# Prompt scores as paired products of 64 rows, and the last pair of gate and up joined inside the down projection

## The chip, the cores and the metric

The kernel runs on one core of a Trainium2 chip. The metric is the device time of one execution in microseconds; the kernel before has a median of 2318.37 us over three runs (2318.06 to 2319.26). The names of the engines are those of the profile: PE is the matrix engine (PEld its weight loads), DVE the vector engine, ACT the scalar engine, POOL and SP the two engines that here issue most transfers (POOL through the software queue q0, SP through the hardware queue q1).

## The reference, cut to what matters

One step of a decoder of two layers, in float32, for a prompt of 1024 positions and eight samples of one position each with 2048 cached positions. Layer 0 mixes with an S5 recurrence and a differential attention, layer 1 with a gated recurrence and pooling; each layer ends with a SwiGLU. The two parts that matter:

```python
# attention of the prompt: 4 heads, each with two components of 64 dimensions
s = jnp.einsum('bqhd,bkhd->bhqk', qblk, k)          # per component
p = jax.nn.softmax(where(causal, s, -inf))
w = p[:, :, 0] - lam * p[:, :, 1]                   # component 0 minus lam times component 1
o = jnp.einsum('bhqk,bkhe->bqhe', w, v)

# each layer's feed-forward part, 1024 -> 2816 -> 1024
return (jax.nn.silu(x @ wg) * (x @ wu)) @ wd
```

The prompt and the samples go through the feed-forward part together: 1024 + 8 = 1032 columns.

## The kernel before

Every large product is made of three products of operands split into a high and a low part (high by high, low by high, high by low), which is what lines 718 to 720 issue. The feed-forward products go further and use a scheme of seven products for a 2 by 2 block. A program of its own sorts the instructions of each engine ahead of the run; each engine then takes its row of instructions in that order and waits in place where an operand isn't there yet.

**The prompt's attention** (some 290 us of the run, from 330 to 620 us) is worked through in eight rounds: four heads with the first 512 query rows (G=0), then the four heads with the second 512 (G=1). A round has four groups of 128 query rows (qi 0 to 3); group qi of round G looks at nk = (4G + qi + 1) * 128 keys, in blocks of at most 512. `attn_load` fetches the q and k of the next round while the current one runs; it is a generator, and `LOADS` says how many of its steps are taken ahead of each group. In memory a head's q and k lie as one high and one low matrix each (`qd[h][i]`, `kd[h][i]`), whose 128 rows are the 64 dimensions of component 0 and, below them, the 64 of component 1. Before, the Q tile holds for each component the high part of q in its upper 64 rows and the low part in its lower 64; KH and KL hold one component's high (low) part of k twice, in the upper and the lower 64 rows (at G=0 both lie in a tile K). So one product of 128 rows by KH gives qh·kh + ql·kh, and one by KL gives qh·kl + ql·kl. `attn_scores` issues these two per block and component (L1308, L1309), then adds the causal mask with a product in bfloat16 (L1311). At G=0 the two components share one PSUM tile of the pool `sc`; at G=1 each has its own, and the pool has two. DVE takes the maxima (L1313 at G=1, L1317 at G=0), ACT the exponentials (L1319); `attn_values` subtracts the components, transposes (L1338) and multiplies by v (L1348).

The same stage carries, in between, the eight samples' attention over the cached values: SP loads pages kv of 256 KB into eight buffers, and PE multiplies them (`so`, L1453). It also carries the output projection: POOL loads residual rows xr and stores the sums xp, ao and az to memory, and its queue is first in, first out; the q and k loads stand in that queue as well.

**The feed-forward part.** `gate_up` makes eleven pairs of gate and up products; after each pair `finish` multiplies the up half by the norm's factors (`normed`, two operations on L404) and joins it with the gate half (two on L409), all four on DVE with 1032 columns each. For the first ten pairs the result goes to memory; the last stays in its tiles `self.last`, which `down` stores when it loads the rest of the residual (`load_x(8)`). `down` begins with operands built on DVE (b, L476 and the sums beside it) and weight sums as and wp: L515 makes the low part of each weight wp. An item is 24 products of PE with one wp.

Of the kernel before, what the change touches and what calls it, by code (L numbers as in the profile page):

```python
# [8 lines left out]
F32 = mybir.dt.float32  # L9
F32R = mybir.dt.float32r  # L10
# [3 lines left out]
ALU = mybir.AluOpType  # L14
AX = mybir.AxisListType
# [18 lines left out]
P, D = "gpsimd", "vector"  # L34
# [23 lines left out]
NB = 16 // NI  # L58
QUEUES = ("gpsimd", "sync", "sync", "gpsimd", "gpsimd")
Y_BUFS = 11  # L60
LOADS = (2, 2, 2, 2)
MID = 4
KV_BUFS = 8
DENSE = (1, 1, 1, 1, 1, 1, 1, 1)
# [132 lines left out]
class Ffn:  # L197
# [180 lines left out]
    def gate_up(self, S, pp):  # L378
        t, nc = self.t, self.t.nc
        pa = t.pd  # L380

        def slots(j):
            return [t.tile("c", pool=None if j else S) for _ in range(2)] + [None, None, set()]
# [18 lines left out]
        def normed(c):  # L402
            for x in c[:2]:
                nc.vector.tensor_tensor(x, x, t.R, ALU.mult)  # L404

        def finish(j, g, u):
            normed(u)
            for i in range(2):
                self.lastf = nc.vector.tensor_tensor(g[i], g[i], u[i], ALU.mult)  # L409
                if j < 10:  # L410
                    nc.gpsimd.dma_start(self.hd[2 * j + i], g[i])
            self.last = g

        cg, cu = slots(0), slots(0)
# [33 lines left out]
        for j in range(1, 11):  # L448
            cg, cu = slots(j), slots(j)
            for v, c in ((0, cg), (1, cu)):  # L450
                w = self.load(v, j, S if v else t.wst)
                got = nxt[2 * j - 2 + v] if 2 * j - 2 + v < AHEAD else None
                for p in ORDER:
                    if p != 2 or got is None:
                        self.product(p, w, c, pp, got=got if p == 1 else None)
                if self.l + v == 0 and j == 5:
                    with t.after(self.lastf):
                        t.lru_consts()
                if v == 0:
                    normed(cg)  # L460
                    for x in cg[:2]:
                        nc.scalar.activation(x, x, AF.Silu)
            finish(j, cg, cu)

    def operands(self, h, grp, S):

# [51 lines left out]
    def down(self, xs, S, pp, chunks):  # L518


        t, nc = self.t, self.t.nc
# [69 lines left out]
        def load_x(n):  # L591
            for m in range(len(xs), n):
                xs.append(t.tile(f"x{m}"))
                nc.sync.dma_start(xs[m], self.xd[m])
# [16 lines left out]
        def prep():  # L611
            ci, grp, p, m = weights.pop(0)
            ms = (m, m + 2) if grp and m % 4 == 0 else (m,)
            for j, mm in enumerate(ms):
                if (ci, grp, mm) not in raws:
                    raws[ci, grp, mm] = raw(ci, mm, grp, j), {}
            if ci + grp == 0 and m == 2 and len(xs) < 8:
                load_x(8)
                for j in range(2):
                    nc.sync.dma_start(self.hd[20 + j], self.last[j])  # L620
            made[ci, grp, p, m] = self.down_weights(p, *raws[ci, grp, m])

        bank, now = {}, None
        for n, (ci, grp, p, m, more) in enumerate(items):
# [6 lines left out]
            last = ci == chunks[-1] and grp == 1  # L631
# [8 lines left out]
class Trunk:  # L640
# [314 lines left out]
    def mixer0(self):  # L955
        tc, nc, a = self.tc, self.nc, self.a
        with ExitStack() as es:
# [17 lines left out]
            with tc.tile_pool(name="smp", bufs=1) as self.kv, ExitStack() as es5:  # L975
# [54 lines left out]
                with tc.tile_pool(name="mix", bufs=8) as self.T:  # L1030
# [9 lines left out]
                    for i, (h, G) in enumerate(order):  # L1040
                        nxt = loads[order[i + 1]] if i < 7 else iter(())
                        for qi in range(4):
                            for _ in range(LOADS[qi]):
                                next(nxt, None)
# [218 lines left out]
    def attn_load(self, h, G):  # L1263

        nc = self.nc
        n = 512 * G + 512
        self.qk = getattr(self, "qk", {})
        Q = self.tile("Q", F32R)[:, :1024].rearrange("p (c n) -> p c n", c=2)
        ks = []
        self.qk[h, G] = (Q, ks)  # L1270
        for half in range(2):
            src = self.qd[h][half][:, G * 512:G * 512 + 512].bitcast(F32R).rearrange("(c p) n -> p c n", c=2)
            nc.gpsimd.dma_start(Q[half * 64:half * 64 + 64], src)
        yield
        for c in range(2):
            if G:
                ks.append([self.tile(t, F32R)[:, :n] for t in ("KH", "KL")])
            else:
                t = self.tile("K", F32R)
                ks.append([t[:, 0:512], t[:, 512:1024]])  # L1280
            for i in range(2):
                for half in range(2):
                    nc.gpsimd.dma_start(ks[c][i][half * 64:half * 64 + 64],
                                        self.kd[h][i][c * 64:c * 64 + 64, :n].bitcast(F32R))
                yield

    def attn_scores(self, h, G, qi):

        nc = self.nc
        Q, ks = self.qk[h, G]  # L1290
        if qi == 0:
            self.sums = getattr(self, "sums", {})
            self.sums[h, G] = self.sm.tile([128, 2, 4], F32, tag="sums", name="sums")
        sm = self.sums[h, G][:, :, qi]
        nk = (4 * G + qi + 1) * 128
        mx = self.sm.tile([128, 2], F32, tag="mx", name="mx")
        both = None if G else self.sc.tile([128, 2, 512], F32, tag="sc", name="sc")
        P2 = None if G else self.tile("P")
        S, P = [], []
        for c in range(2):  # L1300
            KH, KL = ks[c]
            ql = Q[:, c, qi * 128:qi * 128 + 128]
            ps = self.sc.tile([128, 1024], F32, tag="sc", name="sc") if G else both[:, c]
            for k0 in range(0, nk, 512):
                n = min(512, nk - k0)
                last = k0 + n == nk
                o = ps[:, k0:k0 + n]
                nc.tensor.matmul(o, ql, KH[:, k0:k0 + n], start=True, stop=False)  # L1308
                nc.tensor.matmul(o, ql, KL[:, k0:k0 + n], start=False, stop=not last)  # L1309
                if last:  # L1310
                    nc.tensor.matmul(o[:, n - 128:n], self.identb, self.maskb, start=False, stop=True)  # L1311
            if G:
                nc.vector.tensor_reduce(mx[:, c:c + 1], ps[:, :nk], AX.X, ALU.max, negate=True)  # L1313
            S.append(ps[:, :nk])
            P.append(self.tile(f"P{c}")[:, :nk] if G else P2[:, c * 512:c * 512 + nk])
        if not G:
            nc.vector.tensor_reduce(mx, both[:, :, :nk], AX.X, ALU.max, negate=True)  # L1317
        for c in range(2):
            nc.scalar.activation(P[c], S[c], AF.Exp, bias=mx[:, c:c + 1], accum_out=sm[:, c:c + 1])  # L1319
        return P  # L1320
# [729 lines left out]
```

## Time and profile before

| | us |
|---|---|
| median of three runs | 2318.37 |
| profiled execution | 2323.5 |
| its span | 2321.7 |
| PE busy | 2192.2 (94%) |
| DVE busy | 1605.3 (69%) |
| ACT busy | 939.3 (40%) |
| POOL busy | 477.4 (21%) |

A row of the profile gives the busy time of a group of instructions, their mean duration, and the idle time ahead of them with what ended it. A wait is put down to the releaser that came last. Windows give busy time and the granted clock of PE in a stretch (1.00 is 2.4 GHz, 0.50 is 1.2 GHz). Matrix products overlap their neighbours, so what one costs is read from the distance between two starts and not from its duration.

### The profile page before, as it was taken

The numbers are of one execution on the slowest core, as the hardware profiler recorded it, in microseconds if no ns is written. First come the engines' busy times: TensorE is split into PE (matmuls) and PEld (weight loads), VectorE is DVE, ScalarE is ACT, GpSimd is POOL, SyncE is SP. The second block draws the span as 40 slices with busy tenths as digits, with TensorE's granted clock in tenths as the row PEclk, the third lists the DMA queues.
The fourth block names the chain that finished last, engine by engine and source line by source line (L and its number), as shares of the span: only waits on it lengthen the run. The fifth ranks groups of instructions, "written<-read, shape, count | busy, mean of one in ns | idle before, by whom it ended". The sixth has DMA issues, their size and how long they took to land.

```text
span 2321.7 us, 44913 instructions
## 1 busy us (share of the span) xinstructions
PE 2192.2 (94%) x17529; PEld 2061.1 (89%) x17529; DVE 1605.3 (69%) x3045; ACT 939.3 (40%) x1746; POOL 477.4 (21%) x585
## 2 busy tenths in 40 slices
PE   6999888887989999999899999999999999989998
PEld 6978766655789999999899998899899999989997
DVE  7879435445687557566999878654956565689966
ACT  5233234333664333333444365543633333344331
POOL 5232322222103333332000000000233333300001
PEclk8999998988999999999999999999999999999999
DMA  6488978998543222222765331334232122266512
GB/s 225 144 262 290 258 227 250 280 272 223 183 152 128 91 74 83 68 82 90 292 218 167 104 84 42 102 114 138 76 107 83 67 82 83 74 239 218 192 64 74
DMA packets 145798, 348.21 MB, mean 150 GB/s; under 512 B 33513, under 2 KB 40554, under 8 KB 145586
## 3 DMA queue, kind: packets, MB, share of 16 engines
q1 hardware_dynamic: 112514, 247.18, 32.4%
q0 software_dynamic: 32496, 97.64, 13.6%
q8 instruction: 138, 2.26, 0.4%
q14 instruction: 74, 0.61, 0.1%
q10 hardware_dynamic: 576, 0.52, 0.1%
HBM read 281.17 MB, written 64.08 MB: 149 GB/s over the span
## 4 chain that ended last, share of the span: by engine, by line
PE 79%; DVE 9%; DMA 7%; ACT 2%; issue 2%; SPq 1%; POOL 1%; DVEq 0%; ACTq 0%; POOLq 0%
PE pd L718 23%; PE pd L720 22%; PE pd L719 22%; DMA kv<-in_cv 3%; DMA kv<-in_ck 2%; PE so L1453 1%; PE po L1348 1%; PE pss L1402 1%; DVE wp L312 1%; DMA xr<-in_x 1%; PE pg L1918 1%; PE pT L1338 1%; PE sc L1308 1%; PE pv L1253 1%; PE pv L1254 1%
## 5 line engine op out<-in xcount | busy, mean ns | idle before, releaser
L720 PE MATMUL pd<-b,wp 128*128 128x256 f32 (+1 forms) x3496 | 987.7, 283 | 14.4 <-DVE wp L515 13.2
L718 PE MATMUL pd<-b,wp 128*128 128x256 f32 (+1 forms) x3496 | 991.7, 284 | 7.6 <-DVE c L373 3.5
L719 PE MATMUL pd<-b,wp 128*128 128x256 f32 (+1 forms) x3496 | 990.7, 283 | 2.3 <-DVE b L275 2.3
L720 PEld LDWEIGHTS pd<-b,wp 128*128 128x128 f32 x3496 | 662.3, 190 | 15.4 <-DVE wp L515 13.6
L718 PEld LDWEIGHTS pd<-b,wp 128*128 128x128 f32 x3496 | 662.6, 190 | 11.0 <-ACT wp L311 3.4
L719 PEld LDWEIGHTS pd<-b,wp 128*128 128x128 f32 x3496 | 662.8, 190 | 3.1 <-DVE b L275 3.1
L331 POOL TENSOR_TENSOR as<-wst 128x512 f32<-128x512 f32 x80 | 136.2, 1702 | 487.5 <-DVE wp L312 328.2
L718 PE MATMUL pd<-xh,wh 128*128 128x344 f32 x576 | 191.1, 333 | 14.7 <-ACT wh L691 10.2
L375 ACT COPY c<-pd 128x512 f32<-128x512 f32 (+1 forms) x260 | 106.1, 444 | 223.0 <-PE pd L720 222.7
L720 PE MATMUL pd<-xh,wl 128*128 128x344 f32 x576 | 188.1, 329 | 4.8 <-DVE wl L692 4.7
L719 PE MATMUL pd<-xl,wh 128*128 128x344 f32 x576 | 188.6, 328 | 0.0
L373 DVE TENSOR_TENSOR c<-pd,c 128x512 f32<-128x512 f32 (+1 forms) x214 | 93.3, 470 | 127.0 <-PE pd L720 126.8
L311 ACT CAST wp<-as 128x512 fp32r<-128x512 f32 x176 | 108.8, 621 | 173.0 <-PE pd L720 164.5
L312 DVE TENSOR_TENSOR wp<-wst,wp 128x512 fp32r<-128x512 f32 x122 | 105.4, 867 | 103.7 <-ACT wp L311 103.7
L312 DVE TENSOR_TENSOR wp<-as,wp 128x512 fp32r<-128x512 f32 x176 | 140.3, 800 | 28.0 <-ACT wp L311 27.9
L404 DVE TENSOR_TENSOR c<-c,R 128x1032 f32<-128x1032 f32 x88 | 110.4, 1255 | 44.9 <-ACT c L375 44.9
L718 PEld LDWEIGHTS pd<-xh,wh 128*128 128x128 f32 x576 | 110.0, 191 | 19.3 <-ACT wh L691 10.6
L583 DVE TENSOR_TENSOR x<-pd,x 128x512 f32<-128x512 f32 x160 | 108.3, 688 | 17.1 <-PE pd L720 15.8
L720 PEld LDWEIGHTS pd<-xh,wl 128*128 128x128 f32 x576 | 109.5, 191 | 8.7 <-DVE wl L692 5.9
L719 PEld LDWEIGHTS pd<-xl,wh 128*128 128x128 f32 x576 | 109.9, 191 | 2.1 <-issue 0.2
L691 ACT CAST wh<-wst 128x1024 fp32r<-128x1024 f32 x58 | 60.7, 1046 | 116.7 <-PE pd L719 85.4
L692 DVE TENSOR_TENSOR wl<-wst,wh 128x1024 fp32r<-128x1024 f32 x58 | 70.8, 1221 | 48.3 <-ACT wh L691 47.9
(537 smaller groups left out, 4075.1 us busy)
## 6 DMA issues: line engine op xcount, KB each, us to landing
h<-hd SPq DMA_DIRECT2D x82, 516.0 KB, 5.8
kv<-in_ck SPq DMA_DIRECT2D x128, 256.0 KB, 4.2
kv<-in_cv SPq DMA_DIRECT2D x128, 256.0 KB, 6.1
wst<-in_w_d SPq DMA_DIRECT2D x48, 512.0 KB, 4.2
wst<-in_w_g SPq DMA_DIRECT2D x46, 512.0 KB, 4.1
wst<-in_w_up SPq DMA_DIRECT2D x44, 512.0 KB, 3.5
hd<-c POOLq DMA_DIRECT2D x40, 516.0 KB, 3.0
wst<-in_w_o POOLq DMA_DIRECT2D x28, 512.0 KB, 4.0
```

The source lines that it names most:

```text
L311: nc.scalar.copy(W[:, 0], s)
L312: nc.vector.tensor_tensor(W[:, 1], s, W[:, 0].bitcast(F32), ALU.subtract)
L331: (nc.vector if self.first else nc.gpsimd).tensor_tensor(s, x, y, op)
L373: V.tensor_tensor(o, i, o, ALU.add)
L375: A.copy(o, i)
L404: nc.vector.tensor_tensor(x, x, t.R, ALU.mult)
L583: nc.vector.tensor_tensor(y, pt[:, :, :256], y, add)
L691: nc.scalar.copy(H, src)
L692: nc.vector.tensor_tensor(L, src, H.bitcast(F32), ALU.subtract)
L718: mm(p, WH, XH, start=first, stop=False, **kw)
L719: mm(p, WH, XL, start=False, stop=False, **kw)
L720: mm(p, WL, XH, start=False, stop=last, **kw)
```

## The change

In attention, q and k are loaded as they lie in memory: two loads of 128 rows for Q and two for K, where there were two for Q and eight for K. One K tile at G=0 and two at G=1 serve both components. The scores of a block are three products of 64 rows for each component (qh·kh, ql·kh, qh·kl); component 0 uses the upper 64 rows of the array and component 1 the lower 64, and the code issues them in turn. The two masks come at the end. At G=1 both PSUM tiles are taken at once. `LOADS` goes from two steps a group to one; a round has four steps now, one load each, so that the second load of k is asked for in the last group of the round before. In the feed-forward part `finish(10)` is called in `down`, just ahead of `load_x(8)` and the two stores, in both layers.

```diff
-LOADS = (2, 2, 2, 2)
+LOADS = (1, 1, 1, 1)
...
-            finish(j, cg, cu)
+            if j < 10:
+                finish(j, cg, cu)
+        self.finish = lambda: finish(10, cg, cu)
...
             if ci + grp == 0 and m == 2 and len(xs) < 8:
+                self.finish()
                 load_x(8)
...
+        for i in range(2):
+            nc.gpsimd.dma_start(Q[:, i], self.qd[h][i][:, G * 512:G * 512 + 512].bitcast(F32R))
+            yield
+            nc.gpsimd.dma_start(ks[i], self.kd[h][i][:, :n].bitcast(F32R))
+            yield
...
+        for k0 in range(0, nk, 512):
+            n = min(512, nk - k0)
+            last = k0 + n == nk
+            for j, (q, k) in enumerate(((0, KH), (1, KH), (0, KL))):
+                for c in range(2):
+                    r = slice(64 * c, 64 * c + 64)
+                    calls.append(lambda c=c, r=r, q=q, k=k, j=j, k0=k0, n=n, last=last: nc.tensor.matmul(
+                        S[c][:, k0:k0 + n], Q[r, q, sl], k[r, k0:k0 + n], start=j == 0, stop=j == 2 and not last))
         for c in range(2):
...
+            calls.append(lambda c=c: nc.tensor.matmul(S[c][:, nk - 128:nk], self.identb, self.maskb, start=False, stop=True))
+        self.row(calls)
```

`self.row(calls)` asks the sorting program to keep the calls together behind the first one. What it makes of that is seen in the order of the instructions. PE, round G=1 of head 0, last group but one (nk = 896), before; sc is the score tile of one component:

```order
L1308 MATMUL sc_7505<-KH_6898,Q_6895 128x512 [waits Activation_49]
L1309 MATMUL sc_7505<-KL_6899,Q_6895 128x512
L1308 MATMUL sc_7505<-KH_6898,Q_6895 128x384
...
L1309 MATMUL sc_7505<-KL_6899,Q_6895 128x384
...
L1311 MATMUL sc_7505<-maskb_684,identb_686 128x128
L1308 MATMUL sc_7513<-KH_7022,Q_6895 128x512
L1309 MATMUL sc_7513<-KL_7023,Q_6895 128x512
```

and the same group now, where lines have moved by one to three (L1308 and L1309 are now L1310, L1311 is L1313):

```order
L1310 MATMUL sc_7501<-KH_6894,Q_6893 128x512 [waits Activation_49]
L1310 MATMUL sc_7501<-KH_6894,Q_6893 128x512
L1310 MATMUL sc_7501<-KL_6895,Q_6893 128x512
L1310 MATMUL sc_7502<-KH_6894,Q_6893 128x512 [waits Activation_49]
L1310 MATMUL sc_7502<-KH_6894,Q_6893 128x512
L1310 MATMUL sc_7502<-KL_6895,Q_6893 128x512
L1310 MATMUL sc_7501<-KH_6894,Q_6893 128x384
L1310 MATMUL sc_7502<-KH_6894,Q_6893 128x384
```

The first block stands as three products of one component and then three of the other; the second stands in turn. At G=0 all groups stand in turn.

POOL's queue around the start of round G=1 of head 0, before (ao, xp are stores of the attention's output and of the sums, xr loads of the residual, wst weights of the output projection):

```order
L1356 DMA ao2_114<-od_6796 128x512 [waits DMASW6_49,DVE_49]
L1846 DMA xp3_119<-xr_6865 128x1032 [waits DMASW7_49]
L1836 DMA xr_7100<-in_x 128x1032 [waits DMASW0_49,PE_49]
L1283 DMA KL_7023<-kd0_108 64x1024 [waits DMASW1_49]
L1283 DMA KL_7023<-kd0_108 64x1024 [waits DMASW2_49]
L696 DMA wst_9060<-in_w_o0 128x1024 [waits DMASW3_49,Activation_49]
```

and now:

```order
L1838 DMA xr_7094<-in_x 128x1032 [waits DMASW3_49,PE_49]
L1358 DMA ao2_114<-od_6794 128x512 [waits DMASW4_49,DVE_49]
L1838 DMA xr_7213<-in_x 128x1032 [waits PE_49]
L1848 DMA xp4_120<-xr_7094 128x1032 [waits DMASW6_49,DMASW3_49,DVE_49]
L1281 DMA KL_6895<-kd0_108 128x1024 [waits DMASW7_49]
```

The residual load has moved ahead of the store ao2; the load of KL has moved behind a store xp4 that waits for DVE.

DVE at the passage from gate and up to down in layer 0, before (c are the gate and up tiles, wp the weights of down):

```order
L404 TENSOR_TENSOR c_14250<-c_14250,R_139 128x1032 [waits DVE_49]
L484 TENSOR_TENSOR h_14714<-h_14714,h_14712 128x520
L409 TENSOR_TENSOR c_14248<-c_14248,c_14250 128x1032 [waits DVE_49]
L404 TENSOR_TENSOR c_14251<-c_14251,R_139 128x1032 [waits Activation_49]
L476 TENSOR_TENSOR b_14745<-h_14714,b_14745 128x520 [waits Activation_49]
L409 TENSOR_TENSOR c_14249<-c_14249,c_14251 128x1032 [waits DVE_49]
L476 TENSOR_TENSOR b_14752<-h_14732,b_14752 128x512 [waits DMAHW1_49,Activation_49]
L476 TENSOR_TENSOR b_14755<-h_14732,b_14755 128x520 [waits Activation_49]
L482 TENSOR_TENSOR h_14730<-h_14730 128x512 [waits DMAHW0_49]
L515 TENSOR_TENSOR wp_14782<-as_14780,wp_14782 128x512
```

and now, from the first wp of down to its fifth (L515 is now L517, L476 is L478, L583 is L585):

```order
L517 TENSOR_TENSOR wp_14814<-as_14812,wp_14814 128x512
...
L478 TENSOR_TENSOR b_14795<-h_14764,b_14795 128x520 [waits Activation_49]
L517 TENSOR_TENSOR wp_14825<-as_14823,wp_14825 128x512 [waits PE_49]
L404 TENSOR_TENSOR c_14286<-c_14286,R_139 128x1032
L404 TENSOR_TENSOR c_14287<-c_14287,R_139 128x1032
L409 TENSOR_TENSOR c_14284<-c_14284,c_14286 128x1032 [waits DVE_49]
L585 TENSOR_TENSOR x1_14800<-pd_14828,x1_14800 128x512 [waits DMAHW7_49,PE_49]
L409 TENSOR_TENSOR c_14285<-c_14285,c_14287 128x1032 [waits DVE_49]
...
L517 TENSOR_TENSOR wp_14876<-as_14874,wp_14876 128x512 [waits Activation_49]
```

The four operations of the join have moved from ahead of the first wp to between the fourth and the fifth.

## Rows read from the trace of the kernel before

**Rows 1.** Windows of the attention stage: length, busy time by engine, PEclk, DMA share, GB/s

```profile
330.00:460.00 130.00, 106.58 (x638) 76.22 (x631) 63.05 (x155) 49.13 (x133) 36.34 (x65) 0.91 0.96 266
460.00:620.00 160.00, 132.99 (x760) 92.88 (x759) 87.07 (x193) 67.42 (x159) 37.46 (x69) 0.90 0.77 215
```

**Rows 2.** Waits of PE in 330 to 620 us: us in total, times, longest us

```profile
PE so L1453 <- DMA kv<-in_cv: 40.8, 10, 11.6
PE sc L1308 <- ACT P L1319: 4.1, 5, 1.5
```

**Rows 3.** Chain of waits, 330 to 620 us: shares by line, and one piece

```profile
by line: DMA kv<-in_cv 20.7%; PE po L1348 9.0%; PE so L1453 8.8%; PE pd L718 8.1%; PE pd L719 7.5%; PE pd L720 7.2%; DMA xr<-in_x 5.2%; PE sc L1308 5.0%; PE pT L1338 5.0%; PE sc L1309 3.9%; PE psn L801 2.6%; DMA K<-kd 2.2%; issue 2.1%; ACT 
...
458.76 8.06 DMA xr<-in_x
```

**Rows 4.** Transfers issued in 330 to 620 us: count, KB each, median us to landing

```profile
DMA packets 30360, 68.85 MB, mean 237 GB/s; under 512 B 4280, under 2 KB 4280, under 8 KB 30335
...
KH<-kd POOLq DMA_DIRECT2D x16, 256.0 KB, 9.0
KL<-kd POOLq DMA_DIRECT2D x16, 256.0 KB, 9.9
...
K<-kd POOLq DMA_DIRECT2D x24, 128.0 KB, 7.6
```

**Rows 5.** Timeline of PE, a score group at G=1: start, duration, line, tiles

```profile
481.91 0.48 PE L1308 MATMUL sc<-KH,Q 128*128 128x512 f32 x1
482.23 0.40 PE L1309 MATMUL sc<-KL,Q 128*128 128x512 f32 x1
482.47 0.28 PE L1308 MATMUL sc<-KH,Q 128*128 128x256 f32 x1
```

**Rows 6.** Timeline of PE in the S5 part: products of 64 rows

```profile
215.27 0.50 PE L1786 MATMUL py<-H,CL 64*128 64x136 f32 x4
215.70 1.08 PE L1402 MATMUL pss<-kv,qsam 128*32 128x128 f32 x32
216.87 0.50 PE L1788 MATMUL py<-H,CL 64*128 64x136 f32 x2
217.29 0.50 PE L1785 MATMUL py<-U,TG 128*128 128x136 f32 x2
```

**Rows 7.** Waits of POOL's queue in 330 to 620 us

```profile
POOL ao L1356 <- DVE sums L1332: 17.5, 1, 17.5
```

**Rows 8.** Waits of PE in 1090 to 1160 us

```profile
PE pd L720 <- DVE wp L515: 6.6, 1, 6.6
```

**Rows 9.** Page, costliest groups: count | busy, mean ns | idle before, releaser

```profile
L720 PE MATMUL pd<-b,wp 128*128 128x256 f32 (+1 forms) x3496 | 987.7, 283 | 14.4 <-DVE wp L515 13.2
```

**Rows 10.** Timeline of DVE, layer 0, the end of gate and up and the start of down

```profile
1116.22 1.23 DVE L404 TENSOR_TENSOR c<-c,R 128x1032 f32<-128x1032 f32 x1
...
1120.87 1.23 DVE L409 TENSOR_TENSOR c<-c 128x1032 f32<-128x1032 f32 x1
...
1123.82 0.69 DVE L515 TENSOR_TENSOR wp<-as,wp 128x512 fp32r<-128x512 f32 x1
...
1131.07 0.69 DVE L515 TENSOR_TENSOR wp<-as,wp 128x512 fp32r<-128x512 f32 x1
```

**Rows 11.** Timeline of PE at the same passage

```profile
1117.70 0.28 PE L719 MATMUL pd<-b,wp 128*128 128x256 f32 x1
1124.57 0.58 PE L720 MATMUL pd<-b,wp 128*128 128x256 f32 x1 [6.59 <-DVE wp L515]
...
1134.90 0.28 PE L718 MATMUL pd<-b,wp 128*128 128x264 f32 x1
1135.02 0.28 PE L719 MATMUL pd<-b,wp 128*128 128x264 f32 x1
```

**Rows 12.** Window behind that wait, columns as in Rows 1

```profile
1125.00:1130.00 5.00, 5.00 (x30) 5.00 (x30) 5.00 (x10) 0.62 (x1) 0.00 (x0) 0.65 0.99 376
```

More of the change, by code (lines that the diff above doesn't have):

```diff
@@ L1267, in attn_load @@
         self.qk = getattr(self, "qk", {})
-        Q = self.tile("Q", F32R)[:, :1024].rearrange("p (c n) -> p c n", c=2)
-        ks = []
-        self.qk[h, G] = (Q, ks)
[L1271 to L1285, printed above, removed]
+        Q = self.tile("Q", F32R)[:, :1024].rearrange("p (i n) -> p i n", i=2)
+        if G:
+            ks = [self.tile(t, F32R)[:, :n] for t in ("KH", "KL")]
+        else:
+            t = self.tile("K", F32R)
+            ks = [t[:, 0:512], t[:, 512:1024]]
+        self.qk[h, G] = (Q, ks)
+        for i in range(2):
[3 more added lines that the diff above has]
+            yield
     def attn_scores(self, h, G, qi):
         nc = self.nc
-        Q, ks = self.qk[h, G]
+        Q, (KH, KL) = self.qk[h, G]
         if qi == 0:
@@ L1296, in attn_scores @@
         mx = self.sm.tile([128, 2], F32, tag="mx", name="mx")
-        both = None if G else self.sc.tile([128, 2, 512], F32, tag="sc", name="sc")
-        P2 = None if G else self.tile("P")
-        S, P = [], []
-        for c in range(2):
[L1301 to L1315, printed above, removed]
@@ L1316, in attn_scores @@
-        if not G:
+        if G:
+            S = [self.sc.tile([128, 1024], F32, tag="sc", name="sc")[:, :nk] for _ in range(2)]
+            P = [self.tile(f"P{c}")[:, :nk] for c in range(2)]
+        else:
+            both, P2 = self.sc.tile([128, 2, 512], F32, tag="sc", name="sc"), self.tile("P")
+            S = [both[:, c, :nk] for c in range(2)]
+            P = [P2[:, c * 512:c * 512 + nk] for c in range(2)]
+        sl = slice(qi * 128, qi * 128 + 128)
+        calls = []
+        for k0 in range(0, nk, 512):
[6 more added lines that the diff above has]
+                        S[c][:, k0:k0 + n], Q[r, q, sl], k[r, k0:k0 + n], start=j == 0, stop=j == 2 and not last))
@@ L1317, in attn_scores @@
+        for c in range(2):
+            calls.append(lambda c=c: nc.tensor.matmul(S[c][:, nk - 128:nk], self.identb, self.maskb, start=False, stop=True))
+        self.row(calls)
+        if G:
+            for c in range(2):
+                nc.vector.tensor_reduce(mx[:, c:c + 1], S[c], AX.X, ALU.max, negate=True)
+        else:
             nc.vector.tensor_reduce(mx, both[:, :, :nk], AX.X, ALU.max, negate=True)
```

## The prediction

> **What bounds the kernel now.** I read the windows first, since PE's 94% is an average over stages. In the attention stage PE is busy for 106.6 of 130 and 133.0 of 160 us, at granted clocks of 0.91 and 0.90, while the 16 DMA engines are at 0.96 and 0.77 [rows 1]: 50 us of PE time are empty there, and a part of the rest ran at the lower level. The waits of PE say why: 40.8 us in ten waits for pages of cached values, against 4.1 us for a score tile that ACT has not yet emptied [rows 2]. The chain agrees: of these 290 us, 20.7% are transfers of cv, 5.2% of xr and 2.2% of K, 28.1% or 81.5 us together; the rest is mostly PE [rows 3]. So the stage is half one thing and half the other: a saved byte counts where the chain lies on a transfer, and a PE instruction more counts where it lies on PE. No PE wait for q or k stands in the list.
>
> The other place is the passage from gate and up to down. PE stops for 6.6 us until DVE has made the first low weight part [rows 8]; on the page the same pair has 13.2 us, one such wait in each layer [rows 9]. DVE has no gap there, and four operations of 1.23 us of the last join stand ahead of that L515 [rows 10].
>
> **The change part by part.** All sums are made against the profiled execution of 2323.5 us; the median of the runs is 5.1 us below it, and I take the same difference off.
>
> *Bytes.* In the window K, KH and KL are loaded 24 times with 128 KB and 32 times with 256 KB [rows 4]; half of it goes, 1.5 + 4 MB in units of 1024 KB, or 5.8 MB of the 68.85 MB moved, 8.4%. Q stays at 256 KB a load. If every transfer on the chain is shortened in that proportion, 8.4% of 81.5 us is 6.8 us. If the piece that is a K load itself (2.2%, 6.4 us) halves, and the remaining 75.1 us shrink by 8.4%, it is 3.2 + 6.3 = 9.5 us. The upper end is 5.8 MB at the 0.24 to 0.29 MB per us that the stage moves, 20 to 24 us, which is still under the 40.8 us of waits; I use 20. The lower end is 0: eight buffers decide when a page can be asked for. I take 8 us gained, near the two proportional sums, because in the first stretch (370 to 440 us) PE hardly waits for pages and bytes saved there buy nothing.
>
> *Columns of the scores.* Before, four products for each block and 128 query rows: 4 x 18,432 = 73,728 columns. If all products ran in pairs side by side it would be three quarters of that, 55,296. But in the order a group at G=1 has the first block's three products of one component, then three of the other, so only neighbours of different components can overlap. Counted through the order it comes to 69,504. A 512-column product takes 0.24 us from start to start [rows 5], so the 4,224 columns are 2.0 us. The masks now stand together: the product behind a mask takes 0.32 us to the next start and not 0.24 [rows 5], and 32 such places go, 2.6 us. That two products on different halves run at once is seen in the S5 part: four products of 64 rows on two halves take 0.43 us, two on one half 0.42 us [rows 6].
>
> *Changes between 128 and 64 rows.* The same rows show the price: two products of 136 columns take 0.42 us between neighbours of another shape [rows 6], where 264 columns without such a change take 0.12 us each [rows 11], so a change costs at least 0.42 - 0.24 = 0.18 us. The order has 135 changes of shape on PE in the stage where it had 63: 72 more, 13.0 us. PE's net is 13.0 - 2.0 - 2.6 = 8.4 us more. About 0.6 of the stage's chain is PE, and what falls into a wait for pages is free, so I charge 5.1 us; the ends are 0 and 13.
> The Trainium skill, "TensorEngine Tiling (Array Packing)", section "Key Properties", says that changing the tiling mode drains the engine, which speaks against this change; the 0.18 us agrees with it. The same page's "Theoretical Speedup" promises up to two for a contraction of at most 64; taken at its word for all pairs, 18,432 columns or 8.6 us would go and the sum below would be 4.0 us lower.
>
> *Late KL.* The second load of k is now asked for in the last group of the round, one transfer of 512 KB at G=1 behind the store xp4, which waits for DVE. In the order 26 rows of PE stand between the KH products and the KL products of head 0's first group, some 5 us. Two transfers of 256 KB took 9.9 us to land [rows 4]. So a wait of up to 5 us at that place, and the like at three more; but the order before had such a gap for the second component too, and showed no wait. I charge 2 us; the ends are 0 and 20.
>
> *PSUM.* At G=1 both score tiles are needed at once, and the maximum of component 0 starts only behind both masks. The 4.1 us of waits for ACT [rows 2] are the nearest row. I charge 1.5 us more, ends 0 and 4.
>
> *POOL's queue.* Before, the xr load of 458.76 stood behind ao2, which held the queue for 17.5 us [rows 7], and its 8.06 us lie on the chain [rows 3]. Now that load stands ahead of ao2. What is late next is the cv page or KL, so of the 8.06 us I take 1.5, ends 0 and 3. That 48 transfers fewer are issued on POOL is counted as nothing; POOL is busy for 36 of 130 us and waits otherwise [rows 1].
>
> *The join.* The four operations leave the way of the first wp, 4 x some 1.15 us start to start. But PE's first items also need the fourth operand b, which by DVE's new order is ready at about 1123, 1.6 us ahead of the 1124.57 of before [rows 11]; and the fifth wp, which the fourth item of PE needs, stands behind the join, where DVE is as far as before, about 1132.4 against 1131.8 for the old end [rows 10]. PE reaches it sooner and waits some 3 us there. The item that began at 1135.02 [rows 11] begins at 1132.4: 2.6 us a layer, 5.2 us in two. Upper end 6.6 a layer, the whole wait; lower end 0, since the clock behind a stop is low (0.65 in the 5 us behind it [rows 12]) and two stops may cost what one did. The stores of the last pair and the remaining residual loads come later on SP; their first users come behind 10 or more items, so I charge nothing.
>
> *Sum.* -8.0 + 5.1 + 2.0 + 1.5 - 1.5 - 5.2 = -6.1 us. From 2323.5 that is 2317.4 profiled, and 2312.3 as a median.
>
> **The rivals.** *The bytes go through whole* (-20 in place of -8): for it speaks that the stage stands at a DMA share of 0.96 [rows 1], against it that the shares in the middle of the stage stop nobody. 2318.4 - 18.1 = 2300.3.
> *KL becomes the wait.* At each of the four G=1 rounds the KL products stop PE by 5 us, landing time against the rows between: 20 us and not 2. For it speaks the queue order and a transfer twice as large; against it that cv waits shrink meanwhile. 2318.4 - 6.1 + 18 = 2330.3. It decides the sign from 2.7 us a round on, where 10.7 us are met.
> *The halves don't run side by side.* Then 110,592 columns in place of 69,504, 19.3 us more, 0.6 of it on the chain: 2323.9. The S5 rows speak against it; that these have 136 columns and not 512 is what is left for it.
> *The join's gain is given back* at the fifth wp and by the clock: 2317.5.
>
> **How the numbers follow.** A measurement of this kernel tells some 0.2% from no change, 4.6 us: faster means under 2313.7, slower above 2323.0. The forecast gets 0.50, its own range 2306 to 2318, of which 0.33 is under 2313.7 and 0.17 above. Whole bytes 0.20 (0.19 faster). KL 0.13 (slower). Halves one after the other 0.05 (0.03 same, 0.02 slower). Join given back 0.12 (0.11 same, 0.01 faster). Sums: faster 0.53, same 0.32, slower 0.15. The range reaches from 2300, the middle of the first rival, to 2325, in the lower half of the second; about a tenth is left out on either side.
>
> **What would show it.** In the profile after: the DMA of 330 to 620 us at about 63 MB and the waits for cv at some 30 us in place of 40.8; pairs of L1310 that start some 0.01 us apart; 0.18 us or more of extra distance at each change of shape; no PE wait for KL of over 2 us; the stop at the start of down at about 5 us, and a second one of about 3 us for the fifth wp, the fourth item some 2.6 us earlier after the end of gate and up. The forecast is wrong if the cv waits stay at 40 us, if a wait for KL stands in PE's list, or if the second stop at down is as long as what the first one lost.

## The result

The changed kernel takes 2294.13 us (median of four runs, 2292.93 to 2296.49) against 2318.82 us; the ratio is 0.9888, 95% interval 0.9874 to 0.9901. That is 24.7 us less where 6.1 were forecast, and below the range of 2300 to 2325. The sign was right; the size, and with it most of the reasons, was not.

Below, a run is given by its ratio to the kernel before as run on the same chip, since the kernel before itself lay between 2318.8 and 2323.4 us on the chips that were used. One thousandth is 2.3 us. The changed kernel is 0.9888.

### The profile page after: what moved, and what is told of

Read it like the earlier page. It is cut to its first block, busy times and chain, and to the rows that moved or that the text cites. A ratio compares the mean times of both kernels' runs of the same rounds, so it can differ in the third digit from the quotient of the medians.

```text
span 2292.0 us, 45014 instructions
## 1 busy us (share of the span) xinstructions
PE 2191.9 (96%) x17625; PEld 2051.4 (90%) x17625; DVE 1604.4 (70%) x3045; ACT 939.2 (41%) x1746; POOL 450.8 (20%) x537
## 4 chain that ended last, share of the span: by engine, by line
PE 76%; DVE 11%; DMA 5%; issue 5%; ACT 2%; POOL 1%; SPq 1%; DVEq 0%; POOLq 0%; ACTq 0%
PE pd L723 22%; PE pd L721 22%; PE pd L722 22%; DMA kv<-in_ck 2%; PE pss L1404 1%; PE po L1350 1%; DMA kv<-in_cv 1%; DVE wp L312 1%; DMA xr<-in_x 1%; DVE b L478 1%; PE so L1455 1%; PE sc L1310 1%; PE pg L1920 1%; PE pv L1257 1%; PE pv L1256 1%
## 5 line engine op out<-in xcount | busy, mean ns | idle before, releaser
L585 DVE TENSOR_TENSOR x<-pd,x 128x512 f32<-128x512 f32 x160 | 108.4, 688 | 11.6 <-PE pd L723 10.4
L311 ACT CAST wp<-wst 128x512 fp32r<-128x512 f32 x122 | 76.4, 630 | 59.2 <-PE pd L723 56.9
```

The costliest lines, as they stand in the source:

```text
L311: nc.scalar.copy(W[:, 0], s)
L585: nc.vector.tensor_tensor(y, pt[:, :, :256], y, add)
```

## The profile after

The waits of PE in the attention stage (310 to 640 us of the new trace; us in total, times, longest), to be set against [rows 2]:

```profile
PE so L1455 <- DMA kv<-in_cv: 17.4, 5, 5.5
PE pT L1340 <- DVE xr L1844: 4.7, 2, 3.5
...
PE sc L1310 <- ACT P L1321: 1.8, 3, 0.8
...
PE sc L1310 <- DMA KL<-kd: 1.6, 1, 1.6
```

The waits for cached values fell from 40.8 to 17.4 us. The score tile waits for ACT fell too, from 4.1 to 1.8 us, and one wait for KL of 1.6 us is new. The whole stage between the same products of PE, columns as in [rows 1], before:

```profile
310.00:640.00 330.00, 278.23 (x1675) 201.10 (x1673) 165.41 (x379) 140.32 (x339) 75.03 (x135) 0.92 0.84 238
```

and after:

```profile
303.95:618.81 314.86, 282.09 (x1771) 197.72 (x1769) 167.05 (x379) 141.32 (x338) 51.41 (x93) 0.93 0.69 233
```

The stage is 15.1 us shorter. PE stands idle for 32.8 us in it where it was 51.8, but it is busy for 3.9 us longer, at a granted clock that is no lower. The DMA share fell from 0.84 to 0.69. The transfers of k, against [rows 4] (330 to 620 us there, 324 to 600 us here; 64.25 MB are moved in all, for 68.85):

```profile
KH<-kd POOLq DMA_DIRECT2D x4, 512.0 KB, 8.0
KL<-kd POOLq DMA_DIRECT2D x4, 512.0 KB, 6.3
...
K<-kd POOLq DMA_DIRECT2D x6, 256.0 KB, 5.4
```

Set side by side at the same products of PE, the two profiled executions (2321.7 and 2292.0 us of span) part at four places. The new one is 2.1 us behind at 275 us of the old trace and 6.1 us ahead at 290. It is 22.7 us ahead at 660. Then it gains 2.2 us at the passage from gate and up to down in layer 0 (23.1 to 25.3) and 2.9 us in layer 1 (26.6 to 29.5). The profiled run of before was 4.7 us above its median, so some of the 29.7 is luck; the runs below say what is not.

The first of these places I had not looked at. PE's waits there, 225 to 310 us, before:

```profile
PE pss L1402 <- DMA kv<-in_ck: 6.1, 2, 5.5
```

and after:

```profile
PE pss L1404 <- DMA kv<-in_ck: 1.8, 3, 1.0
```

Windows of before around that wait:

```profile
275.00:280.00 5.00, 2.12 (x19) 1.92 (x17) 0.00 (x0) 0.05 (x1) 0.00 (x0) 1.00 1.24 280
280.00:285.00 5.00, 2.37 (x34) 1.89 (x35) 0.00 (x0) 0.27 (x1) 0.00 (x0) 0.70 0.66 206
285.00:290.00 5.00, 5.00 (x32) 3.14 (x33) 1.23 (x1) 1.84 (x3) 0.00 (x0) 0.62 0.66 183
```

PE stands for half of ten us while pages of cached keys come late, and the granted clock behind the stop is 0.62, a mixture of the two levels. The loads of the first round of attention, eight of k and two of q, are issued at 267 to 275 us beside those pages.

## The experiments

**The join alone, and everything but the join.**

```diff
 before
-            finish(j, cg, cu)
+            if j < 10:
+                finish(j, cg, cu)
+        self.finish = lambda: finish(10, cg, cu)
...
+                self.finish()
                 load_x(8)
```

> The kernel before with only the last join of gate and up moved into down. If the 3.4 us a layer that the two traces show at the start of down is the join's own, it takes 5 to 8 us off: 2311 to 2314 us. If a part of the 24.7 us comes from the join by way of the stages behind it, 2309 or less; if the join's gain needs the new attention, 2317 to 2319.

Measured: 0.9987 (0.9972 to 1.0003), ten runs from 2312.6 to 2321.7 us. That is 3 us, with an interval from nothing to 6.5: not settled by the times. At the passages its trace gains 2.3 and 2.8 us on the trace of before, the same sizes as above.

The opposite, the changed kernel with `finish(10)` back in its place:

```diff
-            if j < 10:
-                finish(j, cg, cu)
-        self.finish = lambda: finish(10, cg, cu)
+            finish(j, cg, cu)
...
-                self.finish()
```

> The changed kernel with the last join back in gate and up. If the parts add up, it stands 5 to 8 us above the changed kernel, 2299 to 2302 us, so the attention part alone is worth 17 to 20 us.

Measured: 0.9915 (0.9893 to 0.9936), 2300.7 us. By the ratios the join is worth 6.3 us in the new kernel, though the two intervals overlap a little; the traces' 5.1 us is the firmer number. The attention part is the rest, some 18 to 20 us.

**The old loads under the new products.** The eight transfers of 64 rows are put back; half of the bytes go to a second set of tiles that nobody reads, taken from the same pool of 24, and `LOADS` is two steps again.

```diff
-LOADS = (1, 1, 1, 1)
+LOADS = (2, 2, 2, 2)
...
+            if G:
+                sp = [self.tile(t, F32R)[:, :n] for t in ("KH", "KL")]
+            else:
+                t = self.tile("K", F32R)
+                sp = [t[:, 0:512], t[:, 512:1024]]
...
+        for d in (ks, sp):
+            for i in range(2):
+                for half in range(2):
+                    c = half if d is ks else 1 - half
+                    nc.gpsimd.dma_start(d[i][half * 64:half * 64 + 64],
+                                        self.kd[h][i][c * 64:c * 64 + 64, :n].bitcast(F32R))
+                yield
```

> The changed kernel with q and k fetched as before: eight transfers of 64 rows for k in each round, the second half of the bytes into tiles that nobody reads, two steps ahead of each group, the products still in pairs of 64 rows. Theory of the loads (the bytes and transfers of k hold the pages of cached keys and values up): most of the attention's 17 to 20 us is given back, 2308 to 2314 us, the 5 us wait near 280 us for cached keys returns and PE's waits for cached values are near 40 us. Theory of the products (the pairs and their compact place in PE's order bring the gain): 2293 to 2298 us.

Measured: 0.9997 (0.9978 to 1.0015), 2318.1 us. By the times the whole gain is gone, the join's share too, though the trace still gains 2.1 and 3.0 us at the two passages. PE's waits in the stage and ahead of it:

```profile
PE so L1467 <- DMA kv<-in_cv: 34.2, 9, 7.2
...
PE pss L1416 <- DMA kv<-in_ck: 4.2, 2, 4.0
```

and the stage between the same products of PE as above:

```profile
310.61:641.54 330.93, 288.50 (x1771) 200.82 (x1769) 169.13 (x379) 140.53 (x338) 74.02 (x135) 0.92 0.81 239
```

With the loads of before the new products still leave PE less idle than it was (42.4 us for 51.8), but PE is busy for 288.5 us against 278.2, at the same granted clock of 0.92. So the new products alone bring nothing, and they cost PE time. The gain needs the new loads; but these loads differ in four things at once: bytes, transfers and their shape, tiles held, and how early. The next runs take them apart.

**Bytes.** Each load of k made twice in transfers of 128 rows, the second one into a tile that nobody reads.

```diff
             nc.gpsimd.dma_start(ks[i], self.kd[h][i][:, :n].bitcast(F32R))
+            nc.gpsimd.dma_start(sp[i], self.kd[h][i][:, :n].bitcast(F32R))
             yield
```

> The changed kernel with each load of k made twice, the second time into a tile that nobody reads: as many bytes of k as before, but in transfers of 128 rows, four in a round. If the bytes alone hold the stage: as the run with the old loads, 2311 to 2318 us. If it is the number of transfers and their 64 rows: little above the changed kernel, 2295 to 2302 us.

Measured: 0.9937 (0.9921 to 0.9954), 2306.8 us: 11 us given back, between the two expectations. Either half of the bytes' price, or something else that this run has too. It has: the second set of tiles.

**Places of the pool without bytes.** The same tiles are taken, but only 8 columns are loaded into each of them:

```diff
             nc.gpsimd.dma_start(ks[i], self.kd[h][i][:, :n].bitcast(F32R))
+            nc.gpsimd.dma_start(sp[i][:, :8], self.kd[h][i][:, :8].bitcast(F32R))
             yield
```

> The changed kernel with the second set of k tiles taken from the pool of 24, and only 8 columns loaded into it: the places of before without the bytes. If the freed places of the pool let other loads start earlier, and this is a part of the gain: 2300 to 2312 us. If not: 2293 to 2298 us.

Measured: 0.9947 (0.9931 to 0.9964), 2308.9 us, 14 us given back. Without the bytes it is no faster than with them: 6 MB of loads cost nothing measurable (the two intervals leave room for some 3 us) beyond the places that their tiles take. No run loads these bytes without taking the places, so what they would cost where the pool has room stays open. That the bytes count was the theory on which my forecast's largest gain stood.

Two controls. As many small transfers, but into a tile of its own outside the pool:

```diff
+            nc.gpsimd.dma_start(self.spk[:, 8 * i:8 * i + 8], self.kd[h][i][:, :8].bitcast(F32R))
```

> The changed kernel with two more small loads of k a round (8 columns each) into a tile of its own outside the pool of 24: as many transfers more as in the run that took places of the pool, but no place taken. If that run's 14 us came from the places: 2293 to 2297 us. If they came from more transfers in POOL's queue: 2303 to 2311 us.

Measured: 0.9888 (0.9871 to 0.9904), 2296.2 us: nothing. More transfers in POOL's queue are not the cost. And the places by rounds:

```diff
-        if True:
+        if G == 1:
             if G:
                 sp = [self.tile(t, F32R)[:, :n] for t in ("KH", "KL")]
```

> As the run that took places of the pool, but in the four rounds of G=1 alone, where two tiles more are held (one at G=0). In that run nearly all of the loss came behind 460 us, in these rounds: theory of the places, 2303 to 2309 us. If the loss needs the rounds of G=0 as well, or was luck of the sorting: 2294 to 2299 us.

> The changed kernel with one more tile of the pool held in each of the four rounds of G=0 and 8 columns loaded into it. If places cost by their number, two in three of those of G=1 alone, whose run stood 10 us above: 2297 to 2301 us. If only the rounds of G=1 are short of places: 2293 to 2297 us.

Measured: 0.9911 (0.9892 to 0.993), 2304.5 us with two tiles more in the rounds of G=1, four runs in two pairs (2300.7, 2300.9, 2308.1, 2309.3); 0.9886 (0.9864 to 0.9907), 2295.8 us with one tile more in the rounds of G=0. This points to G=1 as the rounds that are short of places, though the two intervals overlap, and 5 us by the ratio (10 by the medians) is less than the 14 us of both. The trace, of the slowest of the four runs, says the same: at 460 us of the old trace it is 19.2 us ahead, as the changed kernel (19.1), at 640 us 7.7 against 21.2. PE's waits in the stage, first with two tiles more at G=1:

```profile
PE so L1464 <- DMA kv<-in_cv: 25.4, 8, 9.3
```

and then with the small transfers outside the pool:

```profile
PE so L1458 <- DMA kv<-in_cv: 17.0, 4, 5.6
```

A held tile is paid at the pages of cached values: 25.4 us of waits against 17.4, with no byte more. How it gets there isn't settled. A full pool makes loads wait for a place, and it also leads to another order of the instructions; the two were not separated, since the order is made for the pool that it has.

**The first round.** The old eight loads of k in the first round alone:

```diff
+        if h + G == 0:
...
+            for d in (ks, sp) if sp else ():
+                for half in range(2):
+                    c = half if d is ks else 1 - half
+                    nc.gpsimd.dma_start(d[i][half * 64:half * 64 + 64],
+                                        self.kd[h][i][c * 64:c * 64 + 64, :n].bitcast(F32R))
```

> The changed kernel with the old loads of k (eight transfers of 64 rows, half of them into a tile nobody reads) in the first round alone, which are issued near 268 us beside the pages of cached keys. If these make the wait of 5.5 us near 280 us in the kernel before: 2298 to 2302 us, and that wait is back. If that wait is of another cause: 2293 to 2296 us.

Measured: 0.9912 (0.9895 to 0.9928), 2299.4 us. PE's wait for cached keys is back in part:

```profile
PE pss L1417 <- DMA kv<-in_ck: 3.3, 2, 3.1
```

The same products of PE go from 2.2 us ahead of the changed kernel's trace at 260 us to 2.2 us behind at 300. So this place, ahead of the stage in which I made my sums, is worth some 5 us. Whether by bytes, shape or the tile held is not told apart here.

**64 rows.** Each load of k cut into two of 64 rows, no byte and no tile more:

```diff
-            nc.gpsimd.dma_start(ks[i], self.kd[h][i][:, :n].bitcast(F32R))
+            for r in (slice(0, 64), slice(64, 128)):
+                nc.gpsimd.dma_start(ks[i][r], self.kd[h][i][r, :n].bitcast(F32R))
```

> The changed kernel with each load of k cut into two transfers of 64 rows: half the bytes of before, in the shape of before. If the bytes alone count: 2293 to 2297 us. If a transfer of 64 rows costs as much as one of 128: 2304 to 2312 us.

Measured: 0.9950 (0.9932 to 0.9968), median 2305.6 us, five runs from 2293.0 to 2314.7. The run that was profiled is the fastest and its trace looks like that of the changed kernel, so its cause can't be read. A loss as large as that of the held tiles, with no tile held, is thus left unexplained. The next run speaks against a price of the shape: the old loads once more, with all bytes and tiles, but one step ahead.

```diff
-LOADS = (2, 2, 2, 2)
+LOADS = (2, 1, 1, 1)
```

> The changed kernel with the old eight loads of 64 rows for k, half of them into tiles nobody reads, but one step ahead of each group (two ahead of the first). Against the run that loads k twice in 128 rows only the cut into 64 rows differs. If 64 rows cost time of their own: 2312 to 2320 us. If the 11 us between the two earlier runs came from the tiles being taken a group earlier: 2304 to 2309 us.

Measured: 0.9935 (0.9913 to 0.9958), 2306.0 us, the same as with 128 rows (0.9937). Against it the old loads two steps ahead (0.9997) lose 14 us: holding the larger number of tiles earlier costs as much as holding them at all. What the cut alone did in the run ahead of it stays open.

**How early.** In the changed kernel, with its fewer tiles:

```diff
-LOADS = (1, 1, 1, 1)
+LOADS = (2, 2, 2, 2)
```

and all four loads ahead of the first group:

```diff
-LOADS = (1, 1, 1, 1)
+LOADS = (4, 0, 0, 0)
```

> The changed kernel with two steps of the loads ahead of each group in place of one, so that the tiles of the next round are taken and loaded one or two groups earlier. Theory of the places: tiles held longer, 2297 to 2304 us. If early loads are only good (no late KL, 1.6 us of wait): 2290 to 2294 us.

> The changed kernel with all four loads of the next round ahead of its first group. Two steps ahead stood 2 us (median) to 6 us (ratio) below one step. If early loads go on to help while the pool has room: 2285 to 2291 us. If the tiles held for a whole round bring the old shortage back: 2297 to 2310 us.

Measured: two steps ahead 0.9863 (0.9846 to 0.9879), 2291.8 us; all four 0.9896 (0.9879 to 0.9913), 2298.9 us. With room in the pool two steps don't cost, and this is the fastest median of all, though its interval overlaps that of the changed kernel. All four ahead lose against two. And in the kernel before, with its own products:

```diff
-LOADS = (2, 2, 2, 2)
+LOADS = (2, 1, 1, 1)
```

> The kernel before, its old loads and products, with one step of the loads ahead of each group (two ahead of the first) in place of two: the tiles of the next round are taken up to one and a half groups later. If holding tiles of the pool early is what cost in the kernel before, as the runs with the old loads say: 2306 to 2313 us. If that needs the new products: 2316 to 2322 us.

Measured: 1.0005 (0.9991 to 1.0018): no gain at all, a miss. PE's waits in its stage show two new ones beside the old:

```profile
PE so L1453 <- DMA kv<-in_cv: 37.5, 11, 6.3
PE sc L1309 <- DMA KL<-kd: 2.4, 1, 2.4
PE sc L1309 <- DMA K<-kd: 1.7, 1, 1.7
```

So the pool's shortage is not the only thing that holds the old kernel. With the same loads and steps, the new products and the join (0.9935) are 16 us faster; PE there waits 10 us less for pages, 27.5 against 37.5. I have no run that shows why.

**Whose queue.** The loads of q and k issued by SP, and by ACT:

```diff
...
-            nc.gpsimd.dma_start(ks[i], self.kd[h][i][:, :n].bitcast(F32R))
+            nc.sync.dma_start(ks[i].bitcast(F32), self.kd[h][i][:, :n])
...
```

> The changed kernel with the loads of q and k issued by SP, beside the pages, and not by POOL. If what a tile of k costs is that its load waits in POOL's queue ahead of residual loads and stores: 2284 to 2291 us. If SP's pages then wait behind the loads in the same way: 2295 to 2310 us.

> The changed kernel with the loads of q and k issued by ACT's queue. Queue theory as for SP: 2284 to 2291 us. If ACT is held up by a load that waits for its tile, with the exponentials behind it: 2296 to 2310 us.

Measured: 0.9893 (0.9874 to 0.9913) and 0.9936 (0.9913 to 0.9959). SP's queue changes nothing, ACT's costs 11 us. POOL's queue isn't where k's loads hurt.

**PE's time.** First the order of the pairs: three products of one component, then three of the other.

```diff
-            for j, (q, k) in enumerate(((0, KH), (1, KH), (0, KL))):
-                for c in range(2):
+            for c in range(2):
+                for j, (q, k) in enumerate(((0, KH), (1, KH), (0, KL))):
```

> The changed kernel with the three products of component 0 ahead of the three of component 1 in each block, so that only neighbours at the seam can run side by side; nothing else moves by more than a few rows. Of 18432 columns in pairs per product 3 become 5 slots of 6: up to 110592 minus a third, some 14 to 19 us of PE time more than in the changed order, of which 0.6 on the chain: 2301 to 2306 us if PE time in the stage counts. If the transfers alone set the stage's length: 2293 to 2297 us.

Measured: 0.9889 (0.9869 to 0.9909), the changed kernel's time. The reason is in its timeline of PE, a group of 1024 keys:

```profile
478.42 0.74 PE L1310 MATMUL sc<-KH,Q 64*128 64x512 f32 x4
478.99 0.39 PE L1310 MATMUL sc<-KL,Q 64*128 64x512 f32 x2
479.22 0.62 PE L1310 MATMUL sc<-KH,Q 64*128 64x512 f32 x4
```

Six products of 512 columns take 0.80 us (478.42 to 479.22), three times the distance of one and a tenth, and not five times. They start in pairs, four by KH and then two by KL, although in the queue of this group the first products of component 0 stand together ahead of those of component 1. So PE starts products of the two halves out of the order of its queue. My expectation is void: the run didn't take the pairs away. The same group in the changed kernel, queued in turn for its last four products only, and with the same times:

```profile
476.66 0.74 PE L1310 MATMUL sc<-KH,Q 64*128 64x512 f32 x4
...
477.47 0.62 PE L1310 MATMUL sc<-KH,Q 64*128 64x512 f32 x4
477.93 0.39 PE L1310 MATMUL sc<-KL,Q 64*128 64x512 f32 x2
478.25 0.28 PE L1313 MATMUL sc<-maskb,identb 128*128 128x128 bf16 x2
478.37 0.60 PE L1340 MATMUL pT<-ident,P 128*128 128x128 f32 x4
```

From 476.66 to 478.37 the group takes 1.71 us. Before, a group of 1024 keys:

```profile
503.34 0.39 PE L1308 MATMUL sc<-KH,Q 128*128 128x512 f32 x1
...
505.33 0.23 PE L1311 MATMUL sc<-maskb,identb 128*128 128x128 bf16 x1
505.49 1.07 PE L1453 MATMUL so<-kv,ss 128*32 128x512 f32 x8
```

2.15 us. The changed kernel's group is one in which all products pair. In others component 1 has to wait for ACT to empty its score tile, and component 0's products run alone meanwhile. A group of 896 keys of that kind (the one whose order "The change" shows):

```profile
470.48 0.72 PE L1310 MATMUL sc<-KH,Q 64*128 64x512 f32 x2
471.05 0.39 PE L1310 MATMUL sc<-KL,Q 64*128 64x512 f32 x1
471.06 0.73 PE L1310 MATMUL sc<-KH,Q 64*128 64x512 f32 x4
...
472.48 0.28 PE L1313 MATMUL sc<-maskb,identb 128*128 128x128 bf16 x2
```

The end of ACT's exponentials for which component 1 waits there, until 471.01:

```profile
470.81 0.20 ACT L1321 ACTIVATION_READ_ACCUMULATOR P<-sc,mx 128x1 f32 x1
```

And the same group of the next head, queued alike, in which the tile was free:

```profile
503.80 0.74 PE L1310 MATMUL sc<-KH,Q 64*128 64x512 f32 x4
504.36 0.40 PE L1310 MATMUL sc<-KL,Q 64*128 64x512 f32 x2
...
505.22 0.29 PE L1313 MATMUL sc<-maskb,identb 128*128 128x128 bf16 x2
```

It is 2.00 us against 1.42 up to the masks. The second of these groups also starts four products by KH ahead of the first by KL, which stands third in that order. In the last group of the stage the order has all six products of component 0 and its mask ahead of component 1, and each six take 1.58 us, where twelve in pairs took 1.59 above:

```profile
584.46 0.73 PE L1310 MATMUL sc<-KH,Q 64*128 64x512 f32 x2
...
586.04 0.23 PE L1313 MATMUL sc<-maskb,identb 128*128 128x128 bf16 x1
```

Added up over all score and mask records from start to start (a distance over 0.6 us counted as 0.6, since it holds a wait), it is 51.1 us before and 45.3 after. These 5.8 us are not what PE gained. Nine distances were cut off before and five after, so fewer waits are a part of it; and the sum leaves out what the change of shape costs the product ahead of a group. That product takes 0.27 us to the next start where its neighbour of the same size takes 0.17:

```profile
405.07 0.34 PE L722 MATMUL pd<-zl,wh 128*128 128x384 f32 x1
405.24 0.33 PE L723 MATMUL pd<-zh,wl 128*128 128x384 f32 x1
405.51 0.79 PE L1310 MATMUL sc<-K,Q 64*128 64x384 f32 x6
```

Over the whole stage PE is busy for 3.9 us more, as shown above. These are single traces, and PE's busy time depends on the granted clock: with the old products it is 282.5 us at 0.90, in the run with the join alone. At 0.92, where the kernel before has 278.2 us, three runs with the new products (the join put back, the places, the old loads) have 285.7 to 288.5. So the new products cost PE some 4 to 10 us.

Whether PE's time in the stage counts was then asked with more of it:

```diff
-enumerate(((0, KH), (1, KH), (0, KL)))
+enumerate(((0, KH), (1, KH), (1, KH), (1, KH), (0, KL)))
```

> The changed kernel with the product ql by kh issued three times in each block, so the scores hold twice that small term too much: five pairs of products for three, 36864 columns more, 17 us of PE at 0.235 us for 512 columns. If 0.6 of PE's time in the stage is on the path, as my sum had it: 2302 to 2306 us. If PE's time is free there: 2293 to 2297 us.

Measured: 0.9949 (0.993 to 0.9967), 2311.1 us, 14 us more by the ratios. The same sum over its records is 68.6 us, 23.3 more than after. PE's busy time in the stage, between the same products as above, is 300.25 us, 18.2 more. So PE's time counts with 0.6 to 0.8; the prediction had 0.6.

## Why the prediction was wrong

- **Bytes (-8.0).** The effect that I looked for is there, the waits for pages fell from [rows 2]'s 40.8 to 17.4 us, but not for my reason. Bytes on top of held tiles cost nothing (0.9937 with, 0.9947 without), and the tiles alone give 14 us back, where as many transfers without a tile give nothing. The step that failed is the choice of cause: the share of bytes in the window was the only price that I put on the loads. That half of k's tiles were gone from a pool of 24 that nearly everything in the stage shares stands in the diff, and it had no term in the sum. That held tiles cost time is shown; that they are the whole of it is not, since cutting the loads into 64 rows gave 14 us back with no tile held, and in the kernel before holding them later gained nothing.
- **The place of the first round (no term).** I took the stage to begin at 330 us, where the scores begin. Its first loads are issued 60 us earlier, beside the pages of cached keys. Undone alone it gives 5 to 6 us back.
- **PE (+5.1).** The direction was right and the size possible: over the stage PE is busy for 3.9 us more between the two traces and for 7 to 10 us more at a like clock, where 8.4 were forecast; at 0.6 that is 2 to 6 us lost, and 5.1 were charged. Columns: I counted 69,504, since only neighbours in the order were to overlap. That premise was wrong, since products pair up across three or four places of the queue; but where component 1 waits for its tile, and in the last group, they don't. Against groups of the same size that pair, these groups take some 6 us more by my estimate (0.6 us in the one shown, 1.6 in the last), which at 0.23 us for 512 columns is 13,000 columns on top of the 55,296 of full pairing. So the count came out nearly right, by luck. Changes of shape: 0.18 us each was too much. The product ahead of a group takes just under 0.1 us more (405.24), the first pair 0.1 us more than the next ones, and a pair of 512 columns is left for the masks after 0.32 us (477.93 to 478.25) where the next pair would start after 0.23 to 0.24: some 0.28 us for the two changes of a group, 0.14 each. The Trainium skill, "TensorEngine Tiling (Array Packing)", section "Key Properties", says that tiles of the array work independently and that a change of the mode drains it. The traces agree with both, with 0.14 us for a change; that the products need not stand in turn in the queue is from the run with the other order.
- **The join (-5.2).** Right in size, 2.2 and 2.9 us in the traces. Not right in how: the first stop is not 5 us but 1.45, and the second is ended by the sums of the residual that stand on DVE between the two joins. PE's starts behind a wait in layer 0:

```profile
1098.74 0.39 PE L723 MATMUL pd<-b,wp 128*128 128x256 f32 x1 [1.45 <-DVE wp L517]
1104.59 0.38 PE L721 MATMUL pd<-b,wp 128*128 128x256 f32 x1 [2.25 <-DVE x L585]
1108.26 0.39 PE L721 MATMUL pd<-b,wp 128*128 128x256 f32 x1 [0.50 <-ACT wp L516]
```

- **Late KL (+2.0)** is one wait of 1.6 us: right. **PSUM (+1.5)** can't be read from PE's waits for ACT, which fell from 4.1 to 1.8 us: while component 1 waits for its score tile, PE isn't idle but runs component 0's products alone, as at 470.48 (0.6 us there). That price stands in PE's busy time. **POOL's queue (-1.5)** shows no gain in its own name: PE's waits for xr went from 2.8 to 4.7 us in the lists of the two kernels; other engines' part was not followed.
- **The rivals.** Whole bytes (2300.3) came nearest in time, and for the wrong cause. KL as a wait, halves one after the other and a join given back are all excluded by the rows above.

Do the parts add up? Undone one by one from the changed kernel, the places give 14 us, the first round 5.6, the join 5.1 to 6.3; that is 25 to 26 of 24.7, although the changed kernel also carries what PE's longer work costs. Done one by one on the kernel before, the join gives 3 (0 to 6.5) and later loads give nothing. So the parts lean on each other. It would fit that time saved elsewhere in the stage is spent waiting while pages are late, but no run shows it. The sum by parts holds from the new kernel's side only, and why the old products with late loads wait 10 us longer for pages than the new ones is open.

## What to carry to other kernels

When a change drops a tile or a copy, price the place in the pool beside the bytes: hold the same tile with a few columns loaded, and see what of the gain goes. Follow a prefetch to where it is issued, not to where it is used, and look for what it meets there. And where several things share a late transfer, undo parts from the new kernel as well as doing them on the old one, because the two answers differ. Read what a change costs an engine from its busy time between the same instructions on either side, since the records of the changed instructions leave out what their neighbours pay.

## What the runs showed of the hardware

Products on the two halves of 64 rows run side by side also when three or four of one half stand ahead of the other half's in the queue: six products of 512 columns in 0.80 us with that order as well as in turn. That each engine takes its row strictly in order, as the kernel before is described, does not hold for PE here. Where the other half's first product has to wait for its score tile, the products run alone (2.00 us for a group of 896 keys against 1.42). A change of the array's shape costs about 0.14 us, or 0.28 us for the way in and out of a group (at the product ahead of it, at its first pair and ahead of the masks, just under 0.1 us each), where I took 0.18 for each change from the S5 rows [rows 6]. Six more MB of loads into tiles that were held anyway, in a stage with a DMA share of 0.7, cost nothing that could be measured. And executions of one kernel spread by up to 22 us (2293.0 to 2314.7) when only the cut of its k loads was changed, where the changed kernel spreads by 3.6.
